# Causal attention scores without their masked columns, and gate projections placed inside an attention's loop

## The chip, the cores and the metric

The kernel runs on one core of a Trainium2 chip. Its time is device microseconds of one execution, and the time of record is the median of three. The engines are TensorE (PE, with its weight loads shown apart as PEld), VectorE (DVE), ScalarE (ACT), GpSimd (POOL) and SyncE (SP), whose queue issues nearly all DMA.

## The reference

Two blocks of two layers each work on 256 tokens of width 1024. The change is in the second block only, in its token mix, which runs once in each of the two layers: three causal attentions over one input, each with eight heads of 64, then a gated sum.

```python
def _token_mix(h, w_in, ...):
    q_a, kv_a, g_a, q_b, k_b, v_b, q_c, k_c, v_c, f_c = _split_cols(h @ w_in)
    o_a = _nsa(q_a, kv_a, g_a, ...)                 # compressed + selected + window attention
    o_b = _swa_sink(q_b, k_b, v_b, sinks, ...)      # window of 128, with a sink
    o_c = _fox(q_c, k_c, v_c, f_c, b_f)             # full causal, with a forget term
    g = jax.nn.sigmoid(h @ w_gate + b_gate).reshape(B, S, N_BRANCH, D)
    merged = g[:, :, 0] * (o_a @ w_br_a) + g[:, :, 1] * (o_b @ w_br_b) + g[:, :, 2] * (o_c @ w_br_c)
    return merged @ w_out

# in _fox, and with masks of their own in the other two:
    logits = jnp.where(s_idx[None] <= t[:, None], logits, -jnp.inf)
    p = jax.nn.softmax(logits, axis=-1)
    return jnp.einsum('bhqk,bhkd->bhqd', p, v)
```

With 256 tokens in two tiles of 128, a query of the first tile never sees a key of the second, in any of the three.

## The kernel before, in words

Every matrix product is done in three matmuls of split operands (`mm3`, L546 to L549): each float32 operand is kept as a high part and a rest, both of a rounded float32 type. A weight chunk of 128 x 1024 is loaded by SP (`advance`, L344), cast by ACT (L354) to its high part and subtracted by DVE (L356) to its rest. `Weights` holds three raw chunks and, in this part, five split ones; `make_plan` fixes the order of the chunks, and `take` and `done` hand them out and give them back. `natural` (a projection) takes four chunks at once and runs the two token tiles over them, eight `mm3` of 512 columns for each; it gives its chunks back in the second tile's pass. An activation tile in PSUM is split by `split` (ACT L536, DVE L537).

`mix` runs the token mix. Its three attentions are loops over eight units (four head pairs of two heads):

- SWA and FOX go through `simple`, and NSA through a loop of its own (L1879 to L1907).
- A unit's part `soft` computes the scores (L1685, L1686 and in FOX L1689; in NSA L1847 and L1851), the negated minimum (DVE L625), the exponentials (ACT L615, L1863) and the scaling (DVE L621, L1872).
- The loop then transposes a unit's probabilities on PE (L1710; L1883, L1884), splits them into the buffers `pts`, starts `soft` of the next unit, and multiplies the probabilities with the values by `mm3` (in NSA then L1904 for the compressed keys).

Scores and values run over all 256 keys for either query tile; the softmax reads only the valid 128 of the first tile, and the value product reads a zeroed quarter of `pts` in the place of the others.

Other work is put into these loops as filler: generators stand in a queue, and `fill(ns)` steps the first of them until its declared time is used up. In NSA the filler is the second branch (`branch_job(1)`): for each half of 512 output columns the gate projection (`natural`, evacuated by DVE L1770 and ACT L1771) and then the branch's output projection, whose result is multiplied with the gate by DVE (L1789) and added by POOL (L1790). The third branch (`branch_job(2)`) runs behind the NSA loop, with the add on DVE and, for each token tile and half, a step `last` that transposes the result on PE (L1918) and splits it for the next product (`wout`).

A scheduler then orders the instructions of each engine by priority and readiness, so that matmuls that are written later can move forward.

Of the kernel before, what the change touches and what calls it, by code (L numbers as in the profile page):

```python
# [478 lines left out]
class Kern:  # L479
# [979 lines left out]
    def mix(self, l, xh, xl, mid):  # L1459
        nc, fa, ra, d = self.nc, self.fa, self.ra, self.d  # L1460
        V, A, G, PE = nc.vector, nc.scalar, nc.gpsimd, nc.tensor
        ident = self.ident
        vec = self.load(f"vec2{l}")
# [209 lines left out]
        def simple(prep, vh, vl, paired, og, extra):  # L1673
# [5 lines left out]
            def soft(u):  # L1679
# [3 lines left out]
                for qt in range(2):  # L1683
                    qq, o = q[:, qt * P:qt * P + P], bank[:, qt * P:qt * P + S]
                    PE.matmul(o, qq, kh, start=True, stop=False)  # L1685
                    PE.matmul(o, qq, kl, start=False, stop=extra is None)  # L1686
                    if extra:
                        n = P if qt == 0 else S
                        PE.matmul(bank[:, qt * P:qt * P + n], pick[:, h:h + 1].to_broadcast([P, P]), extra[:, 0:n],  # L1689
                                  start=False, stop=True)  # L1690
                sb, ss = sr.next(), self.sm.next()
# [11 lines left out]
            for n, u in enumerate(units):  # L1703
# [7 lines left out]
                p_h, p_l = pts[n % 2]  # L1711
                self.split(bank[:, 0:384], p_h.a[:, P:], p_l.a[:, P:])
                if i == 0 and j < 3:
# [43 lines left out]

        def branch_job(b, og, last=None):
            oh = og[0].rearrange("p (k t) -> p k t", k=4)
            ol = og[1].rearrange("p (k t) -> p k t", k=4)  # L1760
            for h in range(2):
                bg = bgr.next()
                src = (1, 2, 0)[b]
                nc.sync.dma_start(bg, d[f"bgate{l}"][0:1, src * D + h * 512:src * D + h * 512 + 512]
                                  .partition_broadcast(P))
                th = {}

                def gate_evac(t, ps):
                    th[t] = thr.next()
                    V.tensor_tensor(th[t], ps, bg, ALU.add)  # L1770
                    A.activation(th[t], th[t], AF.Tanh, scale=0.5)  # L1771

                yield from self.natural(f"gate{l}", 8 * b + 4 * h, 2, xh, xl, [0, 1], gate_evac)
                cs = [self.W.take(f"br{l}", 4 * b + 2 * h + c) for c in range(2)]
                for t in range(2):
                    ps = self.pg.next()
                    tk = slice(t * P, t * P + P)
                    for k in range(4):
                        hi, lo = cs[k // 2]
                        sl = slice((k % 2) * 512, (k % 2) * 512 + 512)  # L1780
                        self.mm3(ps, oh[:, k, tk], ol[:, k, tk], hi[:, sl], lo[:, sl], k == 0, k == 3)
                        yield 640
                        if t == 1 and k % 2 == 1:
                            self.W.done()
                    ms = m[:, t, h * 512:h * 512 + 512]
                    if b == 0:
                        V.scalar_tensor_tensor(ms, th[t], 1.0, ps, ALU.add, ALU.mult)
                    else:
                        V.scalar_tensor_tensor(th[t], th[t], 1.0, ps, ALU.add, ALU.mult)  # L1789
                        (V if last else G).tensor_tensor(ms, ms, th[t], ALU.add)  # L1790
                        if last:
                            last(t, h)

# [20 lines left out]


        self.push(branch_job(1, og_c))
        W1 = 288
        slb, wib = ra.alloc(4 * W1), ra.alloc(4 * S)
# [22 lines left out]
        def soft(u):  # L1841
            j, i = u
            q, hd = heads[j][i], j + 4 * i
            bs, bw = self.ps.next(), self.ps.next()
            for qt in range(2):
                for z in range(2):
                    PE.matmul(bs[:, 160 * qt:160 * qt + W1], q[:, qt * P:qt * P + P], sl4[:, i, z],  # L1847
                              start=z == 0, stop=z == 1)
            for qt in range(2):
                for z in range(2):  # L1850
                    PE.matmul(bw[:, P * qt:P * qt + S], q[:, qt * P:qt * P + P], wi4[:, i, z],  # L1851
                              start=z == 0, stop=z == 1)
# [23 lines left out]
        for n, u in enumerate(units):  # L1876
# [3 lines left out]
            for k, (s, o, w) in enumerate(((s1, 160, 32), (s2, P, 0))):  # L1880
# [3 lines left out]
                PE.transpose(bank[0:32, 384:512], s1[:, 160 * k:160 * k + 32], ident)  # L1884
                self.split(bank[:, 0:384], pts[k][0].a[:, P:], pts[k][1].a[:, P:])
                cq, bq = slice(k * P, k * P + P), bank[0:32, 384:512]
# [5 lines left out]
            if n + 1 < 8:  # L1892
                soft(units[n + 1])
            self.fill(2500)
            if i == 0:
                self.obank = self.po.next()
            o = self.obank[:, i * S:i * S + S]
            for k in range(2):
                for kt in range(2):
                    r = slice(S - kt * S, 2 * S - kt * S)  # L1900
                    c = slice(k * P, k * P + P)
                    self.mm3(o, vsh[:, kt, c], vsl[:, kt, c], pts[k][0].a[:, r], pts[k][1].a[:, r],
                             k == 0 and kt == 0, False)
# [17 lines left out]

        self.run(branch_job(2, og_a, last))
        for b in (oga, mb, bgr, thr, vec, tiny):
            b.free()
# [38 lines left out]
```

## Time and profile before

| | us |
|---|---|
| median of three runs | 2344.83 |
| lowest, highest | 2343.74, 2349.3 |
| the profiled execution | 2346.41 |
| its span, first to last instruction | 2344.6 |

Over the span PE is busy for 96%, its weight loads for 79%, DVE for 72%, ACT for 53% and POOL for 10%. A stretch of the trace is read as busy time of each engine in it. Since the modelled end of a matmul lies behind the start of the next, the distance between starts tells more about PE's pace than the duration does. Times in the trace count from the span's start.

### The profile page before, as it was taken

What the parts mean: (1) busy time and instruction counts of PE and PEld (TensorE: products, weight loads), DVE (VectorE), ACT (ScalarE), POOL (GpSimd) and SP (SyncE); (2) the same over time, 40 slices, a digit from 0 to 9 for tenths busy, and PEclk for the clock granted to TensorE, in tenths of its full rate; (3) what the DMA queues carried; (4) which work ended last, traced back from release to release, by engine and by line L of the source; (5) the groups of instructions that cost most, each with busy time, mean ns of one, the idle gap of its engine ahead of it and who ended that gap; (6) DMA issues with size and microseconds to landing.
All of it is one profiled execution on the core that took longest, in us unless ns stands there. A gap on an engine that the chain in (4) does not pass through costs nothing.

```text
span 2344.6 us, 32027 instructions
## 1 busy us (share of the span) xinstructions
PE 2261.1 (96%) x11612; PEld 1858.8 (79%) x11612; DVE 1696.6 (72%) x3192; ACT 1249.1 (53%) x2235; POOL 244.0 (10%) x265
## 2 busy tenths in 40 slices
PE   6999899999999999999999999999999999999998
PEld 3888787787778899888877777788788877777887
DVE  6598999677689997655577897755655677897554
ACT  6385673242347864444367785444444376764452
POOL 1302200222220202200000000000000000000000
PEclk9999999999999999999999999999999999999999
DMA  8121224355443335555646435556556545445554
GB/s 321 45 82 41 75 81 135 126 165 168 134 139 110 103 132 171 179 186 180 220 137 205 138 117 173 179 188 197 189 190 219 163 153 184 144 131 179 189 190 134
DMA packets 102975, 362.98 MB, mean 155 GB/s; under 512 B 11936, under 2 KB 13088, under 8 KB 102304
## 3 DMA queue, kind: packets, MB, share of 16 engines
q1 hardware_dynamic: 102816, 360.93, 46.5%
q8 instruction: 91, 1.49, 0.3%
q14 instruction: 68, 0.56, 0.1%
HBM read 359.84 MB, written 1.05 MB: 154 GB/s over the span
## 4 chain that ended last, share of the span: by engine, by line
PE 55%; DVE 8%; ACT 4%; DMA 3%; issue 2%; POOL 1%; DVEq 0%; ACTq 0%; POOLq 0%; SPq 0%
PE bank L547 17%; PE bank L549 17%; PE bank L548 16%; DVE ra_t L356 2%; ACT ra_t L354 1%; DMA fa_t<-in_gate 1%; PE bank L1402 1%; DVE ra_t L537 1%; DVE fa_t L625 1%; DVE fa_t L1339 1%; DMA fa_t<-in_n 1%; PE bank L1265 1%; ACT ra_t L536 1%; POOL fa_t L543 0%; ACT fa_t L1863 0%
## 5 line engine op out<-in xcount | busy, mean ns | idle before, releaser
L547 PE MATMUL bank<-ra_t 128*128 128x512 f32 (+1 forms) x3216 | 1186.9, 371 | 14.3 <-DVE fa_t L786 5.0
L549 PE MATMUL bank<-ra_t 128*128 128x512 f32 (+1 forms) x3216 | 1172.8, 366 | 8.3 <-DVE ra_t L537 3.8
L548 PE MATMUL bank<-ra_t 128*128 128x512 f32 (+1 forms) x3216 | 1174.6, 367 | 3.8 <-DVE ra_t L537 1.3
L356 DVE TENSOR_TENSOR ra_t<-fa_t,ra_t 128x1024 fp32r<-128x1024 f32 x583 | 722.2, 1241 | 349.1 <-ACT ra_t L354 333.6
L354 ACT CAST ra_t<-fa_t 128x1024 fp32r<-128x1024 f32 x606 | 633.2, 1048 | 602.2 <-PE bank L549 284.5
L547 PEld LDWEIGHTS bank<-ra_t 128*128 128x128 f32 x3216 | 605.4, 189 | 129.1 <-ACT ra_t L536 15.4
L549 PEld LDWEIGHTS bank<-ra_t 128*128 128x128 f32 x3216 | 605.6, 189 | 108.7 <-DVE ra_t L537 7.3
L548 PEld LDWEIGHTS bank<-ra_t 128*128 128x128 f32 x3216 | 607.2, 189 | 103.1 <-DVE ra_t L356 5.1
L865 DVE SCALAR_TENSOR_TENSOR fa_t<-fa_t 128x512 f32<-128x512 f32 (+1 forms) x240 | 161.5, 673 | 6.0 <-ACT fa_t L863 2.8
L537 DVE TENSOR_TENSOR ra_t<-bank,ra_t 128x512 fp32r<-128x512 f32 (+5 forms) x234 | 131.2, 568 | 44.0 <-ACT ra_t L536 41.1
L536 ACT CAST ra_t<-bank 128x512 fp32r<-128x512 f32 (+5 forms) x234 | 112.8, 488 | 84.8 <-PE bank L549 33.4
L543 POOL TENSOR_TENSOR fa_t<-fa_t 128x1 f32<-128x1 f32 (+2 forms) x54 | 69.0, 1278 | 762.3 <-DVE fa_t L542 762.1
L625 DVE CUSTOM_DVE_ANT_0 fa_t<-bank,fa_t 128x256 f32<-128x256 f32 (+2 forms) x320 | 117.0, 396 | 8.7 <-PE bank L1231 1.9
L615 ACT ACTIVATE fa_t<-fa_t 128x257 f32<-128x257 f32 (+5 forms) x160 | 91.5, 574 | 21.4 <-DVE fa_t L625 20.1
L1410 ACT ACTIVATE fa_t<-bank 128x256 f32<-128x256 f32 x88 | 33.9, 385 | 112.5 <-PE bank L549 112.4
L356 POOL TENSOR_TENSOR ra_t<-fa_t,ra_t 128x1024 fp32r<-128x1024 f32 x23 | 58.0, 2520 | 276.1 <-ACT ra_t L354 273.0
L1412 DVE TENSOR_TENSOR fa_t<-fa_t,bank 128x256 f32<-128x256 f32 x88 | 36.8, 418 | 65.7 <-ACT fa_t L1410 65.5
L1184 DVE SCALAR_TENSOR_TENSOR fa_t<-fa_t 128x512 f32<-128x512 f32 x98 | 71.0, 757 | 2.3 <-DMA fa_t<-in_ada 2.0
L1053 POOL TENSOR_TENSOR fa_t<-fa_t 128x512 f32<-128x512 f32 (+1 forms) x32 | 37.3, 1172 | 154.4 <-DVE fa_t L1052 154.4
L638 DVE TENSOR_TENSOR ra_t<-bank,ra_t 64x256 fp32r<-64x256 f32 (+1 forms) x96 | 43.5, 455 | 8.3 <-ACT ra_t L637 5.3
L649 POOL CAST ra_t<-fa_t 64x256 fp32r<-64x256 f32 (+3 forms) x40 | 24.0, 606 | 241.4 <-PE bank L1597 69.9
L1863 ACT ACTIVATE fa_t<-fa_t 128x32 f32<-128x32 f32 (+2 forms) x96 | 39.0, 409 | 14.5 <-DVE fa_t L625 13.9
(218 smaller groups left out, 1701.9 us busy)
## 6 DMA issues: line engine op xcount, KB each, us to landing
fa_t<-in_f1w SPq DMA_DIRECT2D x132, 512.0 KB, 4.2
fa_t<-in_f2w SPq DMA_DIRECT2D x132, 512.0 KB, 4.3
fa_t<-in_tr SPq DMA_DIRECT2D x88, 512.0 KB, 3.5
fa_t<-in_n SPq DMA_DIRECT2D x56, 512.0 KB, 3.6
fa_t<-in_ada SPq DMA_DIRECT2D x48, 512.0 KB, 4.5
fa_t<-in_gate SPq DMA_DIRECT2D x48, 512.0 KB, 3.7
fa_t<-in_nat SPq DMA_DIRECT2D x36, 512.0 KB, 4.2
fa_t<-in_proj SPq DMA_DIRECT2D x24, 512.0 KB, 3.5
```

Source lines behind the costliest of these rows:

```text
L354: nc.scalar.copy(hi, raw)
L356: eng.tensor_tensor(lo, raw, hi.bitcast(F32), ALU.subtract)
L536: self.nc.scalar.copy(hi, src)
L537: self.nc.vector.tensor_tensor(lo, src, hi.bitcast(F32), ALU.subtract)
L543: self.nc.gpsimd.tensor_tensor(out, out, self.nhalf[:, :n], ALU.pow)
L547: mm(ps, lh, rh, start=start, stop=False)
L548: mm(ps, lh, rl, start=False, stop=False)
L549: mm(ps, ll, rh, start=False, stop=stop)
L615: nc.scalar.activation(s[:, :width or n], s[:, :width or n], AF.Exp, bias=mneg, scale=-1.0, accum_out=r)
L625: self.nc.vector.tensor_tensor_reduce(out=out, in0=a, in1=b, op0=ALU.add, op1=ALU.min, scale=-1.0, scalar=init, accum_out=acc)
L865: V.scalar_tensor_tensor(y4, src, w, y4, ALU.mult, ALU.add)
L1184: V.scalar_tensor_tensor(acc[s].a, wk, self.sc[:, kt, s:s + 1], acc[s].a, ALU.mult, ALU.add)
```

## The change

1. In all three attentions the score matmuls of the first query tile run over the 128 keys that it can see (in NSA's first product 32 compressed ones and 128), and the value product of the second key tile covers the second query tile only. `pts` shrinks to three quarters, and its zeroing goes.
2. `branch_job` is taken apart into `gate_half` and `out_half`. The two gate halves of the third branch are pushed into the queue of fillers behind the second branch, before the NSA loop, with a buffer of their own (`ga`); behind the loop only the output halves run.
3. The two `fill` calls of the NSA loop grow from 2500 and 1000 to 4500 and 2300.
4. The plan's order of weight chunks follows: the eight gate chunks of the third branch, then its four output chunks.

```diff
-        for b in range(3):
+        for b in range(2):
             ...
             for h in range(2):
                 add(f"gate{l}", 8 * b + 4 * h, 8 * b + 4 * h + 4)
                 add(f"br{l}", 4 * b + 2 * h, 4 * b + 2 * h + 2)
+        add(f"gate{l}", 16)
+        add(f"br{l}", 8)
...
-        pts = []
-        for i in range(2):
-            b = (ra.alloc(512), ra.alloc(512))
-            for z in b:
-                V.tensor_copy(z.a[:, 0:P], self.zero[:, 0:P])
-            pts.append(b)
+        pts = [(ra.alloc(3 * P), ra.alloc(3 * P)) for _ in range(2)]
...
                 for qt in range(2):
-                    qq, o = q[:, qt * P:qt * P + P], bank[:, qt * P:qt * P + S]
-                    PE.matmul(o, qq, kh, start=True, stop=False)
-                    PE.matmul(o, qq, kl, start=False, stop=extra is None)
+                    n = P if qt == 0 else S
+                    qq, o = q[:, qt * P:qt * P + P], bank[:, qt * P:qt * P + n]
+                    PE.matmul(o, qq, kh[:, :n], start=True, stop=False)
+                    PE.matmul(o, qq, kl[:, :n], start=False, stop=extra is None)
...
-                o = self.obank[:, i * S:i * S + S]
-                for kt in range(2):
-                    r = slice(S - kt * S, 2 * S - kt * S)
+                for kt, r in enumerate((slice(P, 3 * P), slice(0, P))):
+                    o = self.obank[:, i * S + kt * P:i * S + S]
                     self.mm3(o, vh[:, kt, c], vl[:, kt, c], p_h.a[:, r], p_l.a[:, r], kt == 0, kt == 1)
...
+        def gate_half(b, h, th):
+            bg = bgr.next()
+            ...
+            def evac(t, ps):
+                V.tensor_tensor(th[t], ps, bg, ALU.add)
+                A.activation(th[t], th[t], AF.Tanh, scale=0.5)
+            yield from self.natural(f"gate{l}", 8 * b + 4 * h, 2, xh, xl, [0, 1], evac)
+
+        def out_half(b, h, th, og, last=None):
+            ...                       # the rest of branch_job's loop, as it was
+
+        def branch_job(b, og):
             for h in range(2):
+                th = [thr.next(), thr.next()]
+                yield from gate_half(b, h, th)
+                yield from out_half(b, h, th, og)
...
         self.push(branch_job(1, og_c))
+        gab = fa.alloc(4 * 512)
+        ga = gab.v("p (h t c) -> p h t c", h=2, t=2)
+        for h in range(2):
+            self.push(gate_half(2, h, [ga[:, h, t] for t in range(2)]))
...
             for qt in range(2):
+                n = P if qt == 0 else S
                 for z in range(2):
-                    PE.matmul(bs[:, 160 * qt:160 * qt + W1], q[:, qt * P:qt * P + P], sl4[:, i, z],
+                    PE.matmul(bs[:, 160 * qt:160 * qt + 32 + n], q[:, qt * P:qt * P + P], sl4[:, i, z, :32 + n],
                               start=z == 0, stop=z == 1)
...
-            self.fill(2500)
+            self.fill(4500)
...
-            self.fill(1000)
+            self.fill(2300)
...
-        self.run(branch_job(2, og_a, last))
+        for h in range(2):
+            self.run(out_half(2, h, [ga[:, h, t] for t in range(2)], og_a, last))
```

What the scheduler makes of it shows at three places, all in layer 0. On PE, in the middle of the NSA loop, the transposes of a unit (from `fa_t`, into `bank_69` and `bank_68`) were followed by the next unit's scores (into `bank_66`) mixed with the unit's own values (into `bank_70`) and with filler (512 columns). Before:

```order
L547 MATMUL bank_65<-ra_t 128x512
L1883 MATMUL bank_69<-fa_t 128x128 x3
L1884 MATMUL bank_69<-fa_t 32x128
L1883 MATMUL bank_68<-fa_t 128x128 x3
L1884 MATMUL bank_68<-fa_t 32x128
L1847 MATMUL bank_66<-ra_t 128x288 x2
L547 MATMUL bank_70<-ra_t 128x256
L1847 MATMUL bank_66<-ra_t 128x288 x2
L548 MATMUL bank_65<-ra_t 128x512
```

and now:

```order
L551 MATMUL bank_65<-ra_t 128x512
L1891 MATMUL bank_69<-fa_t 128x128 x3
L1892 MATMUL bank_69<-fa_t 32x128
L1891 MATMUL bank_68<-fa_t 128x128 x3
L1892 MATMUL bank_68<-fa_t 32x128
L1854 MATMUL bank_66<-ra_t 128x160 x2
L1854 MATMUL bank_66<-ra_t 128x288 x2
L1859 MATMUL bank_67<-ra_t 128x128 x2
L1859 MATMUL bank_67<-ra_t 128x256 x2
L549 MATMUL bank_65<-ra_t 128x512
```

The values have moved away from the transposes: 24 filler matmuls now stand between the scores and them, and 12 more behind them, from the unit with index 2 on; in the first units the order is close to the old one.

On DVE, behind the NSA loop, a step of the third branch is a multiply from PSUM (L1789, now L1785), an add (L1790, now L1786) and, behind the transposes, a split (L537, now L539 of 128x4x128); L356 splits weight chunks, and L1770 is a gate's evacuation. Before:

```order
L537 TENSOR_TENSOR ra_t<-bank_70,ra_t 64x256
L1770 TENSOR_TENSOR fa_t<-bank_63,fa_t 128x512
L356 TENSOR_TENSOR ra_t<-fa_t,ra_t 128x1024
L537 TENSOR_TENSOR ra_t<-bank_70,ra_t 64x256
L1789 SCALAR_TENSOR_TENSOR fa_t<-fa_t,bank_64 128x512
L1790 TENSOR_TENSOR fa_t<-fa_t 128x512
L356 TENSOR_TENSOR ra_t<-fa_t,ra_t 128x1024
```

and now:

```order
L539 TENSOR_TENSOR ra_t<-bank_70,ra_t 64x256 x2
L1785 SCALAR_TENSOR_TENSOR fa_t<-fa_t,bank_63 128x512
L1786 TENSOR_TENSOR fa_t<-fa_t 128x512
L1785 SCALAR_TENSOR_TENSOR fa_t<-fa_t,bank_64 128x512
L356 TENSOR_TENSOR ra_t<-fa_t,ra_t 128x1024
L539 TENSOR_TENSOR ra_t<-bank_68,ra_t 128x4x128
L1786 TENSOR_TENSOR fa_t<-fa_t 128x512
L356 TENSOR_TENSOR ra_t<-fa_t,ra_t 128x1024
L1785 SCALAR_TENSOR_TENSOR fa_t<-fa_t,bank_65 128x512
```

The gate evacuations are gone from between the steps, and the steps of the four quarters follow one another directly, with 11 to 17 matmuls between their groups of transposes on PE.

On SP, the loads for the end of the NSA loop and the tail (`in_ln` is the next norm's vectors, `in_bgate` a gate's bias). Before:

```order
L344 DMA fa_t<-in_gate 128x1024 x4
L1764 DMA fa_t<-in_bgate 128x512
L344 DMA fa_t<-in_br 128x1024
L1328 DMA fa_t<-in_ln 128x1024
L344 DMA fa_t<-in_br 128x1024
```

and now:

```order
L344 DMA fa_t<-in_gate 128x1024 x4
L1758 DMA fa_t<-in_bgate 128x512
L344 DMA fa_t<-in_gate 128x1024 x4
L344 DMA fa_t<-in_br 128x1024 x2
L1330 DMA fa_t<-in_ln 128x1024
```

The second half's gate chunks have moved ahead of the first half's output chunks.

## Rows read from the trace of the kernel before

**Rows 1.** Busy by stretch: us, then PE, PEld, DVE, ACT, POOL (instructions), PEclk, DMA.
```profile
1345.00:1424.50 79.50, 76.30 (x432) 61.68 (x431) 71.85 (x243) 60.42 (x188) 6.15 (x4) 1.00 0.39 127
1424.50:1455.00 30.50, 30.18 (x141) 24.40 (x141) 23.40 (x29) 15.96 (x20) 0.00 (x0) 1.00 0.58 196
2020.00:2099.00 79.00, 75.77 (x427) 61.24 (x426) 71.31 (x243) 59.98 (x188) 6.16 (x4) 1.00 0.39 126
2099.00:2125.00 26.00, 25.87 (x119) 20.69 (x120) 19.58 (x24) 13.54 (x17) 0.00 (x0) 1.00 0.60 190
```
**Rows 2.** PE in order of time, a dense stretch: start us, duration us, instruction.
```profile
1338.06 0.39 PE L547 MATMUL bank<-ra_t 128*128 128x512 f32 x1
...
1339.88 0.39 PE L549 MATMUL bank<-ra_t 128*128 128x512 f32 x1
```
**Rows 3.** PE in order of time, scores of one FOX unit in layer 0.
```profile
1301.28 0.28 PE L1686 MATMUL bank<-ra_t 128*128 128x256 f32 x1
1301.40 0.22 PE L1689 MATMUL bank<-ra_t 128*128 128x128 f32 x1
1301.46 0.33 PE L1685 MATMUL bank<-ra_t 128*128 128x256 f32 x1
1301.63 0.28 PE L1686 MATMUL bank<-ra_t 128*128 128x256 f32 x1
1301.75 0.28 PE L1689 MATMUL bank<-ra_t 128*128 128x256 f32 x1
```
**Rows 4.** PE's weight loads in order of time, the same scores, first and last.
```profile
1301.16 0.19 PEld L1686 LDWEIGHTS bank<-ra_t 128*128 128x128 f32 x1
...
1301.75 0.19 PEld L548 LDWEIGHTS bank<-ra_t 128*128 128x128 f32 x1
```
**Rows 5.** PE groups by shape, 1345 to 1424.5 us: count, busy, mean ns, idle before.
```profile
L547 PE MATMUL bank<-ra_t 128*128 128x512 f32 x63 | 25.3, 401 | 0.0
L549 PE MATMUL bank<-ra_t 128*128 128x512 f32 x63 | 24.9, 396 | 0.0
L548 PE MATMUL bank<-ra_t 128*128 128x512 f32 x62 | 24.4, 393 | 0.0
L547 PE MATMUL bank<-ra_t 128*128 128x256 f32 x32 | 9.8, 307 | 0.3 <-DVE ra_t L537 0.2
...
L1883 PE MATMUL bank<-fa_t 128*128 128x128 f32 x48 | 7.7, 277 | 2.2 <-DVE fa_t L1872 2.2
L1847 PE MATMUL bank<-ra_t 128*128 128x288 f32 x32 | 6.3, 304 | 0.0
L1851 PE MATMUL bank<-ra_t 128*128 128x256 f32 x32 | 5.4, 282 | 0.0
L1884 PE MATMUL bank<-fa_t 128*32 128x128 f32 x16 | 4.4, 273 | 0.0
L1904 PE MATMUL bank<-ra_t 128*128 128x256 f32 x8 | 2.9, 360 | 0.2
L1659 PE MATMUL bank<-fa_t 128*128 128x128 f32 x12 | 2.2, 282 | 0.5 <-ACT ra_t L665 0.4
```
**Rows 6.** PE's waits in the same stretch: us, times, longest.
```profile
PE bank L1883 <- DVE fa_t L1872: 2.2, 3, 0.9
```
**Rows 7.** PE in order of time, a wait in the SWA stage of layer 0.
```profile
1246.93 0.35 PE L1685 MATMUL bank<-ra_t 128*128 128x256 f32 x1 [1.04 <-DVE fa_t L625]
```
**Rows 8.** DVE groups by shape in the tail, 1424.5 to 1455 us.
```profile
L356 DVE TENSOR_TENSOR ra_t<-fa_t,ra_t 128x1024 fp32r<-128x1024 f32 x12 | 14.7, 1222 | 5.2 <-ACT ra_t L354 4.8
...
L1790 DVE TENSOR_TENSOR fa_t<-fa_t 128x512 f32<-128x512 f32 x4 | 2.8, 688 | 0.1
L1789 DVE SCALAR_TENSOR_TENSOR fa_t<-fa_t,bank 128x512 f32<-128x512 f32 x4 | 2.7, 681 | 0.8 <-PE bank L549 0.8
```

More of the change, by code (lines that the diff above doesn't have):

```diff
@@ L1683, in soft @@
                 for qt in range(2):
-                    qq, o = q[:, qt * P:qt * P + P], bank[:, qt * P:qt * P + S]
-                    PE.matmul(o, qq, kh, start=True, stop=False)
-                    PE.matmul(o, qq, kl, start=False, stop=extra is None)
+                    n = P if qt == 0 else S
+                    qq, o = q[:, qt * P:qt * P + P], bank[:, qt * P:qt * P + n]
+                    PE.matmul(o, qq, kh[:, :n], start=True, stop=False)
+                    PE.matmul(o, qq, kl[:, :n], start=False, stop=extra is None)
                     if extra:
-                        n = P if qt == 0 else S
-                        PE.matmul(bank[:, qt * P:qt * P + n], pick[:, h:h + 1].to_broadcast([P, P]), extra[:, 0:n],
-                                  start=False, stop=True)
+                        PE.matmul(o, pick[:, h:h + 1].to_broadcast([P, P]), extra[:, 0:n], start=False, stop=True)
                 sb, ss = sr.next(), self.sm.next()
@@ L1711, in simple @@
                 p_h, p_l = pts[n % 2]
-                self.split(bank[:, 0:384], p_h.a[:, P:], p_l.a[:, P:])
+                self.split(bank[:, 0:384], p_h.a, p_l.a)
                 if i == 0 and j < 3:
@@ L1756, in mix @@
         thr = Ring(fa, 512, 2)
-        def branch_job(b, og, last=None):
+        def gate_half(b, h, th):
+            bg = bgr.next()
+            src = (1, 2, 0)[b]
+            nc.sync.dma_start(bg, d[f"bgate{l}"][0:1, src * D + h * 512:src * D + h * 512 + 512]
+                              .partition_broadcast(P))
+            def evac(t, ps):
+                V.tensor_tensor(th[t], ps, bg, ALU.add)
+                A.activation(th[t], th[t], AF.Tanh, scale=0.5)
+            yield from self.natural(f"gate{l}", 8 * b + 4 * h, 2, xh, xl, [0, 1], evac)
@@ L1759, in branch_job @@
+        def out_half(b, h, th, og, last=None):
             oh = og[0].rearrange("p (k t) -> p k t", k=4)
             ol = og[1].rearrange("p (k t) -> p k t", k=4)
-            for h in range(2):
[L1762 to L1792, printed above, removed]
@@ new lines, in out_half @@
+            cs = [self.W.take(f"br{l}", 4 * b + 2 * h + c) for c in range(2)]
+            for t in range(2):
+                ps = self.pg.next()
+                tk = slice(t * P, t * P + P)
+                for k in range(4):
+                    hi, lo = cs[k // 2]
+                    sl = slice((k % 2) * 512, (k % 2) * 512 + 512)
+                    self.mm3(ps, oh[:, k, tk], ol[:, k, tk], hi[:, sl], lo[:, sl], k == 0, k == 3)
+                    yield 640
+                    if t == 1 and k % 2 == 1:
+                        self.W.done()
+                ms = m[:, t, h * 512:h * 512 + 512]
+                if b == 0:
+                    V.scalar_tensor_tensor(ms, th[t], 1.0, ps, ALU.add, ALU.mult)
+                else:
+                    V.scalar_tensor_tensor(th[t], th[t], 1.0, ps, ALU.add, ALU.mult)
+                    (V if last else G).tensor_tensor(ms, ms, th[t], ALU.add)
+                    if last:
+                        last(t, h)
@@ L1845, in soft @@
             for qt in range(2):
+                n = P if qt == 0 else S
                 for z in range(2):
-                    PE.matmul(bs[:, 160 * qt:160 * qt + W1], q[:, qt * P:qt * P + P], sl4[:, i, z],
+                    PE.matmul(bs[:, 160 * qt:160 * qt + 32 + n], q[:, qt * P:qt * P + P], sl4[:, i, z, :32 + n],
                               start=z == 0, stop=z == 1)
             for qt in range(2):
+                n = P if qt == 0 else S
                 for z in range(2):
-                    PE.matmul(bw[:, P * qt:P * qt + S], q[:, qt * P:qt * P + P], wi4[:, i, z],
+                    PE.matmul(bw[:, P * qt:P * qt + n], q[:, qt * P:qt * P + P], wi4[:, i, z, :n],
                               start=z == 0, stop=z == 1)
@@ L1884, in mix @@
                 PE.transpose(bank[0:32, 384:512], s1[:, 160 * k:160 * k + 32], ident)
-                self.split(bank[:, 0:384], pts[k][0].a[:, P:], pts[k][1].a[:, P:])
+                self.split(bank[:, 0:384], pts[k][0].a, pts[k][1].a)
                 cq, bq = slice(k * P, k * P + P), bank[0:32, 384:512]
@@ L1898, in mix @@
             for k in range(2):
-                for kt in range(2):
-                    r = slice(S - kt * S, 2 * S - kt * S)
+                for kt, r in enumerate((slice(P, 3 * P), slice(0, P))):
                     c = slice(k * P, k * P + P)
-                    self.mm3(o, vsh[:, kt, c], vsl[:, kt, c], pts[k][0].a[:, r], pts[k][1].a[:, r],
+                    self.mm3(o[:, kt * P:], vsh[:, kt, c], vsl[:, kt, c], pts[k][0].a[:, r], pts[k][1].a[:, r],
                              k == 0 and kt == 0, False)
@@ L1920, in last @@
             self.split(bank.rearrange("p (k t) -> p k t", k=4), m4[:, 0][c], m4[:, 1][c])
-        self.run(branch_job(2, og_a, last))
-        for b in (oga, mb, bgr, thr, vec, tiny):
+        for h in range(2):
+            self.run(out_half(2, h, [ga[:, h, t] for t in range(2)], og_a, last))
+        for b in (oga, gab, mb, bgr, thr, vec, tiny):
             b.free()
```

## The prediction

> **What bounds the kernel now.** I read the busy shares by stretch first. The last attention of a layer's second block (the loop over eight units that ends at L1907, here called the NSA stage) takes 79.5 us in layer 0 and 79.0 in layer 1; the third branch behind it (the tail) takes 30.5 and 26 up to the cuts chosen [rows 1]. In the NSA stage PE is busy for 76.3 of 79.5 us, but DVE for 71.85, which is 90%; in the tail PE is busy for 30.2 of 30.5 and DVE for 23.4, 77%. So the stage has the two engines side by side near their limits, and the tail is PE's alone.
>
> Matmul ends are modelled, so busy PE says little about how much of it is a stream. I therefore count. A 512-column matmul starts every 0.2275 us when nothing stands in the way (eight steps in 1.82 us) [rows 2]. Those of 256 columns start every 0.12, and the weight loads in front of them every 0.118 (five steps in 0.59) [rows 3, 4]. With 0.2275 for the 512-column ones, 0.118 for all of 256 columns and fewer and 0.135 for 288 (0.12 and 32 columns at the slope below), the matmuls of the NSA stage of layer 0 [rows 5] come to 188 x 0.2275 + 212 x 0.118 + 32 x 0.135 = 42.8 + 25.0 + 4.3 = 72.1 us. **The stage holds 7.4 us in which PE doesn't stream.** Layer 1 has five instructions fewer and is 0.5 us shorter, so about the same; 15 us in both. Part of it has a name: the transposes of a unit (L1883) wait for the scaled probabilities (DVE, L1872), 2.2 us in three waits, the longest 0.9 us [rows 6]; the rest are restarts behind the splits, which the modelled durations cover up.
>
> The Trainium skill ("Trainium Kernel Development and Optimization", section Performance Expectations) says to judge PE by the busy share of weight loads and not of matmuls. By that the stage would have 79.5 - 61.7 = 17.8 us of room [rows 1], and both stages 35; the trace doesn't bear that out, since a load also sits idle under a 512-column stream that is itself the limit.
>
> **The narrower matmuls.** Per unit, the SWA and FOX attentions narrow two score and three value matmuls from 256 to 128 columns: 5 x 8 units x 2 attentions x 2 layers = 160. NSA narrows two scores from 288 to 160, two from 256 to 128 and six value matmuls: 10 x 8 x 2 = 160. By columns each would save 128 x (0.2275 - 0.12)/256 = 0.054 us, 17 us in all. But FOX already has a 128-column matmul in a row of 256-column ones (L1689, sixteen of them): it starts 0.06 us before its successor, and the successor then takes 0.17 instead of 0.12 [rows 3]. The four matmuls of that row take 0.47 us, where four at 0.12 would take 0.48. What sets the pace is the weight load, one per matmul, at 0.118 whatever the columns. So 288 of them save 0.005 to 0.01 us, and the 32 from 288 columns 0.017: 1.9 to 3.4 us. I take **2.5 us**, of which 0.8 in each NSA stage, with 0 as the far end. They can't cost anything themselves: the loads are the same and the streams shorter. On DVE eight clearing copies disappear from stretches where PE leads; nothing.
>
> The narrowing also lets the scheduler put the SWA stage in another order, with the same instructions. One wait there, of a score matmul for a softmax's first pass (L625), is 1.04 us long [rows 7]; such a wait may go or double. I take 0, and 1 us either way for each layer.
>
> **The moved gates.** Two halves of four gate chunks, 96 matmuls of 512 columns per layer, now stand in the filler, and the filler calls grow from 3.5 to 6.8 us per unit. This is less of a move than it reads: of the 144 matmuls of the second branch and the 96 gates, 240 in all, 188 already ran inside the NSA stage [rows 5], because the scheduler pulled gates of the third branch forward. So 52 more enter: 52 x 0.2275 = 11.8 us of PE work, which the tail loses. Time is won only where the work goes into the 7.4 us without a stream.
>
> With no wait left, the stage would take 72.1 + 11.8 - 0.8 = 83.1 us where stage and moved work take 79.5 + 11.8 = 91.3 now. But DVE comes along: 52/12 = 4.3 more chunks to split at 1.22 us (L356) and three more gate evacuations at 0.68 (like L1789, the same size) [rows 8] make 71.85 + 5.3 + 2.0 = 79.2 us, 95% of 83.1. If PE can only go so fast that DVE stays at today's 90.4%, the stage takes 79.2/0.904 = 87.6, and the waits that go are 91.3 - 87.6 - 0.8 = 2.9 us. So between 2.9 and 7.4 us of waits go per layer. The new order says where: from the third unit on, the transposes of a unit are followed at once by the next scores, then by 24 filler matmuls, then by the values, then by 12 more, where they used to be followed by values that wait for the split. Such a unit takes PE 36 x 0.2275 + 29 x 0.118, some 11.6 us, against 79.2/8 = 9.9 on DVE, so it should not wait. In units 0 to 2 the order is still nearly the old one, transposes soon after scores, and there the waits on L1872 stay. I leave 3.5 us of waits per layer, so **3.9 us go, twice: 7.8 us**. This is nearer to the end by DVE's share, which is the row for the same engine in the same stage.
>
> SP's queue carries the same loads; the last four br chunks now come behind eight gate chunks in a row. Each is held back by a split that frees its buffer, and there are five split chunks ahead of PE; I cost it at nothing, since 2.7 us of matmuls (12 x 0.2275) stand on each chunk. The cover is gone where DVE falls behind with the splits, and then it is the 95% above that speaks.
>
> **The tail.** What is left is four steps of 12 matmuls and four transposes, 12 x 0.2275 + 4 x 0.118 = 3.2 us each. Each step's chain is DVE's: multiply 0.68, add 0.69, then transposes, then a split of the same size, 0.69, and in the new order about one chunk split, 1.22, between them [rows 8]: 3.28 us. Before, gates stood between the halves and hid this. Now DVE is late by some 0.1 us per step, and the first step also waits for the last unit's output to be split: **0.5 us per layer, 1 us lost**. The bounds: nothing lost; or a second chunk split in every step, 4 x 1.22 x 2 = 9.8.
>
> **Sum.** -2.5 - 7.8 + 1.0 = -9.3 us. The profiled execution took 2346.4 us with a span of 2344.6 and the runs have a median of 2344.8; I take the same off each: 2335.5.
>
> **Rivals.**
> (a) Narrow matmuls pay by columns: -17 for them instead of -2.5, in all 2344.8 - 17 - 6.8 = 2321. For it speaks that 320 of them stand next to one another in pairs, which L1689 never did; against it that the loads of [rows 4] keep 0.118 straight through the narrow one. It decides if two narrow ones in a row start less than 0.1 us apart. The Trainium skill ("TensorE: Matmul & The Clock Gate", section on the back-to-back issue gap) gives about 81 ns for a pair of load and 128-column matmul; by it 320 x 0.039 = 12.5 us would be saved instead of 2.5. The row says 0.118, and the same sentence's 131 ns for 512 columns is not seen here either (0.2275).
> (b) DVE takes the gain back: the chunk splits in the NSA stage come late, and gate matmuls wait for L356 where transposes waited for L1872. Then only the narrowing and 1 to 2 us of waits are left: 2344.8 - 3.5 = 2341. For it: 95%.
> (c) The tail loses its cover outright: transposes directly behind their chain, so that PE waits for multiply, add and a chunk split, 0.68 + 0.69 + 1.22 = 2.6 us, in each of eight steps, 21 us, less 10.3 gained: 2355, slower than before. It decides when DVE needs more than 3.2 + 1.3 us a step, that is with two or three chunk splits in it. Against it: the new order has one in most steps and 11 to 17 matmuls between the groups of transposes.
> (d) The waits all go: 14.8 instead of 7.8, 2344.8 - 16.3 = 2328.5.
>
> **How the numbers follow.** A measurement can tell 0.3%, 7 us, from no change: faster means below 2337.8. My forecast (2331 to 2340) has 0.58, (a) 0.06, (b) 0.20, (c) 0.06, (d) 0.10. Of the forecast about three quarters lie below 2337.8; with (a) and (d) that makes 0.6 faster. The rest of the forecast and (b) make 0.35 within 0.3%, and (c) 0.05 slower. The range leaves out (a), (c) and the edges: 2328 to 2343.
>
> **What would show it.** Right: in the NSA stage nearly all L1883 waits beyond unit 2 gone, about 240 matmuls of 512 columns inside it and the stage about 87 us long; the score and value matmuls of 128 columns starting every 0.11 to 0.12 us; the tail about 14 us. Wrong: pairs of narrow matmuls at 0.06 us (then a); PE waiting for L356 in the NSA stage with DVE above 95% (b); L1918 waiting more than 1 us each time (c).

## The result, and the profile after

The changed kernel is slower: 2367.4 us (median; 2365.4 to 2375.25) beside 2345.32 for the kernel before, a ratio of 1.0098, 95% interval 1.0072 to 1.0124. The profiled execution took 2366.89 us with a span of 2365.1, 20.5 us more than before's. I had forecast 2335.5 and a range up to 2343.

Line numbers have moved by a few: `mm3` is L549 to L551, `split` L538 and L539, scores L1684 to L1687 (NSA L1854, L1859), transposes of SWA and FOX L1707, of NSA L1891 and L1892, the pair transposes of `q_pair` L1657 (L1659 before), copies to `pc` L1895 to L1897, scaling L623 and L1880, and the compressed values L1911.

First the stretches, as busy time of the engines: us, then PE, PEld, DVE, ACT, POOL (instructions), PEclk, DMA. SWA (from 10 us ahead of its first score) and FOX (up to the first NSA score) of layer 0, first before, then after:

```profile
1211.70:1291.50 79.80, 75.78 (x420) 59.27 (x418) 62.36 (x145) 61.07 (x137) 5.90 (x17) 1.00 0.57 185
1291.50:1350.80 59.30, 57.80 (x309) 45.82 (x308) 48.09 (x128) 42.03 (x97) 1.86 (x5) 1.00 0.43 142
...
1208.60:1291.10 82.50, 75.88 (x416) 57.92 (x414) 62.37 (x143) 60.24 (x135) 5.73 (x17) 1.00 0.55 184
1291.10:1354.40 63.30, 59.34 (x313) 47.03 (x312) 49.85 (x129) 43.20 (x99) 1.88 (x5) 1.00 0.38 127
```

And of after the NSA stage and the tail of layer 0, cut as in [rows 1] (from 5.8 us ahead of the first NSA score):

```profile
1348.60:1447.60 99.00, 89.25 (x494) 74.24 (x493) 79.95 (x252) 68.25 (x196) 5.11 (x4) 0.98 0.42 138
1447.60:1464.00 16.40, 16.40 (x80) 13.13 (x79) 13.87 (x19) 8.23 (x11) 0.00 (x0) 1.00 0.46 153
```

SWA and FOX, which I had costed at nothing, are 2.7 and 4.0 us longer, and NSA with its tail 99.0 + 16.4 = 115.4 where [rows 1] have 79.5 + 30.5 = 110.0: 5.4 us longer. That is 12.1 in layer 0; layer 1 repeats it within 0.5 us. Twice 12 are 24, and 3 of them don't show in the span, because the untouched work ahead of SWA was 3.1 us quicker in this execution (SWA begins at 1208.6 instead of 1211.7): the kernel before had two stretches at a lower clock there (granted 0.56 from 464.5 to 468.0 us, 0.55 from 587.4 to 590.8) that this execution lacks.

Where PE waited shows in its waits (us, times, longest). FOX of layer 0, before:

```profile
PE bank L1710 <- DVE fa_t L621: 0.8, 2, 0.6
```

FOX after, and behind the cut NSA after, both in layer 0:

```profile
PE bank L1707 <- DVE fa_t L623: 1.8, 2, 1.4
PE bank L1657 <- ACT ra_t L667: 0.7, 2, 0.4
PE bank L1684 <- ACT ra_t L667: 0.7, 2, 0.4
...
PE bank L1657 <- ACT ra_t L1897: 4.6, 3, 2.3
PE bank L1891 <- DVE fa_t L1880: 2.1, 3, 0.9
PE bank L549 <- ACT ra_t L538: 1.0, 1, 1.0
```

All of PE's waits in FOX add up to 3.8 us now and to 1.4 before, and five matmuls of 512 columns (1.1 us) moved from SWA into FOX; together that is most of its 4.0 us.

The waits of NSA's transposes for the scaling, whose end was the point of the move, are as long as before (2.1 us, [rows 6] have 2.2). New is a wait of the pair transposes for the copies to `pc`, 4.6 us. The longest of them in order of time (start, duration, instruction), on PE, ACT and DVE:

```profile
1406.30 0.39 PE L550 MATMUL bank<-ra_t 128*128 128x512 f32 x1
1409.02 0.44 PE L1657 MATMUL bank<-fa_t 128*128 128x128 f32 x2 [2.34 <-ACT ra_t L1897]
...
1404.41 2.00 ACT L354 CAST ra_t<-fa_t 128x1024 fp32r<-128x1024 f32 x2
1406.43 0.86 ACT L538 CAST ra_t<-bank 128x384 fp32r<-128x384 f32 x2
1408.72 0.25 ACT L1897 CAST ra_t<-bank 32x128 fp32r<-32x128 f32 x1
...
1405.49 1.22 DVE L356 TENSOR_TENSOR ra_t<-fa_t,ra_t 128x1024 fp32r<-128x1024 f32 x1 [0.65 <-ACT ra_t L354]
1406.75 0.69 DVE L1785 SCALAR_TENSOR_TENSOR fa_t<-fa_t,bank 128x512 f32<-128x512 f32 x1
1407.36 1.02 DVE L539 TENSOR_TENSOR ra_t<-bank,ra_t 128x384 fp32r<-128x384 f32 x2
```

The unit's transposes (from 1403.56) fill both PSUM banks of the ring `pt`, and the pair transposes, written right behind them, need the first of the two again. Its readers are a split and the three copies to `pc`, and these stand on ACT behind two weight casts and on DVE behind a weight split and a gate's multiply. In the new order only the scores and five filler matmuls lie between. The wait costs more than its length; PE's clock behind it (the same columns as the stretches):

```profile
1409.00:1411.00 2.00, 1.98 (x7) 1.65 (x8) 1.94 (x12) 1.95 (x10) 0.00 (x0) 0.64 0.20 72
1411.00:1413.00 2.00, 2.00 (x6) 1.52 (x6) 1.87 (x5) 1.62 (x7) 0.00 (x0) 0.51 0.00 0
1413.00:1416.00 3.00, 3.00 (x18) 2.57 (x17) 2.17 (x9) 0.00 (x0) 0.00 (x0) 1.00 0.53 175
```

Behind this wait the granted clock is at its lower level, 1.2 GHz, for some 3.4 us; nine matmuls of 512 columns take 3.6 us there, where [rows 2] give 9 x 0.2275 = 2.05, so 1.6 us more. (The last section has waits as long as this one that no lower clock followed.)

### The profile page after: what moved, and what is told of

The parts are those of the page before. It is cut to its first block, busy times and chain, and to the rows that moved or that the text cites. A ratio compares the mean times of both kernels' runs of the same rounds, so it can differ in the third digit from the quotient of the medians.

```text
span 2365.1 us, 32045 instructions
## 1 busy us (share of the span) xinstructions
PE 2258.1 (95%) x11612; PEld 1857.9 (79%) x11612; DVE 1697.5 (72%) x3184; ACT 1248.1 (53%) x2235; POOL 243.7 (10%) x265
## 4 chain that ended last, share of the span: by engine, by line
PE 51%; DVE 11%; ACT 5%; DMA 3%; issue 3%; POOL 1%; DVEq 0%; ACTq 0%; POOLq 0%; SPq 0%
PE bank L551 16%; PE bank L549 16%; PE bank L550 16%; DVE ra_t L356 3%; ACT ra_t L354 2%; DVE ra_t L539 1%; DVE fa_t L627 1%; PE bank L1404 1%; DVE fa_t L867 1%; DVE ra_t L640 1%; DMA fa_t<-in_br 1%; DVE fa_t L623 1%; ACT fa_t L1871 1%; DVE fa_t L1341 1%; DMA fa_t<-in_n 1%
## 5 line engine op out<-in xcount | busy, mean ns | idle before, releaser
L549 PE MATMUL bank<-ra_t 128*128 128x512 f32 (+1 forms) x3216 | 1184.0, 370 | 18.7 <-DVE fa_t L788 5.0
L551 PE MATMUL bank<-ra_t 128*128 128x512 f32 (+1 forms) x3216 | 1174.0, 366 | 9.1 <-DVE ra_t L539 3.8
L356 DVE TENSOR_TENSOR ra_t<-fa_t,ra_t 128x1024 fp32r<-128x1024 f32 x583 | 720.3, 1238 | 368.9 <-ACT ra_t L354 353.5
L549 PEld LDWEIGHTS bank<-ra_t 128*128 128x128 f32 x3216 | 605.7, 189 | 129.6 <-ACT ra_t L538 16.3
L551 PEld LDWEIGHTS bank<-ra_t 128*128 128x128 f32 x3216 | 606.6, 189 | 110.6 <-DVE ra_t L539 7.3
L539 DVE TENSOR_TENSOR ra_t<-bank,ra_t 128x512 fp32r<-128x512 f32 (+5 forms) x234 | 130.3, 566 | 43.9 <-ACT ra_t L538 42.4
L538 ACT CAST ra_t<-bank 128x512 fp32r<-128x512 f32 (+5 forms) x234 | 112.2, 487 | 81.9 <-PE bank L551 27.4
L627 DVE CUSTOM_DVE_ANT_0 fa_t<-bank,fa_t 128x256 f32<-128x256 f32 (+2 forms) x320 | 115.4, 395 | 7.2 <-PE bank L1233 1.9
L356 POOL TENSOR_TENSOR ra_t<-fa_t,ra_t 128x1024 fp32r<-128x1024 f32 x23 | 57.4, 2494 | 276.6 <-ACT ra_t L354 273.5
L639 ACT CAST ra_t<-bank 64x256 fp32r<-64x256 f32 (+1 forms) x96 | 37.4, 392 | 13.3 <-DVE ra_t L640 4.0
```

What stands on the lines that cost most here:

```text
L356: eng.tensor_tensor(lo, raw, hi.bitcast(F32), ALU.subtract)
L538: self.nc.scalar.copy(hi, src)
L539: self.nc.vector.tensor_tensor(lo, src, hi.bitcast(F32), ALU.subtract)
L549: mm(ps, lh, rh, start=start, stop=False)
L551: mm(ps, ll, rh, start=False, stop=stop)
L627: self.nc.vector.tensor_tensor_reduce(out=out, in0=a, in1=b, op0=ALU.add, op1=ALU.min, scale=-1.0, scalar=init, accum_out=acc)
```

## The experiments

**Which part costs what.** Four kernels take the change apart. Theory A: the narrow matmuls cost the time through the order that the scheduler makes of them. B: the move of the gates does. C: the narrow matmuls are slow in themselves. For NSA, A1 names the wait of the pair transposes, A2 the narrow matmuls.

`narrow_simple` is the kernel before with, in `simple` alone:

```diff
-                    PE.matmul(o, qq, kh, start=True, stop=False)
+                    PE.matmul(o, qq, kh[:, :n], start=True, stop=False)
...
-                    r = slice(S - kt * S, 2 * S - kt * S)
+                for kt, r in enumerate((slice(2 * P, 4 * P), slice(P, 2 * P))):
+                    o = self.obank[:, i * S + kt * P:i * S + S]
```

> The kernel before, with the narrow score and value matmuls in SWA and FOX alone; NSA and the gates as they were. Theory A (the narrow matmuls bring another order on PE, in which the units of SWA and FOX stand closer together, with less filler between a softmax and its transposes): the whole loss of these two stages is here. In the traces of before and after the way from 10 us ahead of the first SWA score to the first NSA score is 139.0 and 145.8 us in layer 0, 138.7 and 145.5 in layer 1, so this kernel takes 2345 + 13.6 = 2359 us, with waits of the transposes for the scaling of 1.4 to 1.8 us per stage. Theory B (the gates' move costs it all: chunks come in another order, and the loads and splits are late): the same as before or 1 to 3 us less, 2342 to 2345. Theory C (narrow matmuls are slow in themselves): their starts lie more than 0.12 us apart.

`after_wide_simple` is the changed kernel with this hunk turned round.

> The changed kernel with SWA and FOX set back to wide matmuls; NSA is narrow, and the gates stand in the filler. Theory A: the two stages take 139 us again, and the loss of NSA and tail is left. From the first NSA score to 12 us behind the last transposes it was 114.6 us before and 119.9 after in layer 0, so this kernel takes 2345 + 2 x 5.3 = 2355 to 2356 us, with three waits per layer of L1657's transposes (the next pair of queries) for the copies to pc, 4.6 us. Theory B (the gates' move costs it all): 2366 to 2368, as the changed kernel.

`gates` is the kernel before with parts 2 to 4 of the change and none of part 1.

> The kernel before with the gates moved and the larger fills, all matmuls wide as before. In its order the pair transposes of the queries stand 11 filler matmuls behind a unit's transposes once and 7 filler matmuls behind the scores once, where the changed kernel has 4 and 5. Theory A1 (in NSA the loss is the wait of these transposes for a PSUM bank that the copies to pc release last): the waits are shorter, one to 1.3 us per layer less each, and the loss is about half, 2345 + 5 = 2350. Theory A2 (the loss of NSA comes with its narrow matmuls, as in SWA and FOX): 2345 or less, down to my first forecast for the moved gates, 2338. Theory B (the move costs it all): 2366.

`after_q_late` is the changed kernel with

```diff
-            if i == 0 and j < 3:
-                heads[j + 1] = q_pair(qa, j + 1)
             if n + 1 < 8:
                 soft(units[n + 1])
             self.fill(4500)
+            if i == 0 and j < 3:
+                heads[j + 1] = q_pair(qa, j + 1)
```

> The changed kernel, with the call of q_pair (the two transposes L1657 and their split for the next pair of queries) written behind the fill of 4500 and not ahead of the next scores; the same instructions. Theory A1: the three waits of L1657 per layer (4.6 us) go, and with them the 3.4 us at a granted clock of about 0.5 behind the longest of them in layer 0 (1.7 us lost there): 2 x 6.3 = 12.6 us less than the changed kernel, 2355. Rival (ACT and DVE are behind with the splits in any case): the same time is waited at the values for their split, 2366 to 2368.

Measured, as ratios to the kernel before: `narrow_simple` 1.0058 (1.0043 to 1.0073), `after_wide_simple` 1.0033 (1.0022 to 1.0043), `gates` 0.9984 (0.9974 to 0.9994), `after_q_late` 1.0057 (1.0042 to 1.0072). So 14 of the 22 us come with the narrow matmuls of SWA and FOX, and 8 with NSA and the gates together. The move by itself is a gain, so B falls, and the 8 must come with NSA's narrow matmuls, which speaks for A2. A1 is right as well, but for part of it. The NSA loop of layer 0 in the changed kernel, then with `q_pair` behind the fill:

```profile
1354.40:1447.30 92.90, 83.55 (x467) 69.90 (x466) 75.69 (x245) 63.70 (x185) 5.11 (x4) 0.98 0.40 130
...
1358.70:1446.30 87.60, 83.33 (x467) 70.04 (x466) 75.22 (x245) 63.31 (x185) 5.16 (x4) 0.98 0.44 138
```

That is 5.3 us (in layer 1 it is 4.1), where I had expected 6.3. Some of it is waited at the values for their split instead, as the rival had it: 1.7 us in one wait of layer 0, 1.0 in the changed kernel.

The narrow matmuls alone in NSA, without the gates:

> The kernel before with narrow matmuls in NSA alone. In its order 78 filler matmuls stand between the last NSA product and the third branch's first transposes where 30 stood before, so 48 fewer lie inside the loop. Theory A (the narrow matmuls make the scheduler pack a loop too closely, here too): slower, by waits of the values for their split and of the transposes for the scaling, some 3 to 6 us per layer: 2352 to 2358. Rival (in NSA the narrow matmuls cost something only together with the moved gates): 2343 to 2346.

1.0058 (1.0036 to 1.0081), 14 us and above my range; the rival falls. That is more than the 8 us of NSA and the gates together, so next to narrow matmuls too the moved gates seem to take time off and not to add any (from the first NSA score to the last transposes of layer 0: 109.7 us here, 106.5 in `after_wide_simple`; the intervals of the two ratios overlap). The parts alone, 14 and 14 us lost and 4 gained, add up to 24; the whole change loses 22. Its waits in the NSA loop of layer 0:

```profile
PE bank L1885 <- DVE fa_t L1874: 6.2, 6, 2.6
```

Here the transposes wait 6.2 us for the scaling where [rows 6] have 2.2; in this order 78 filler matmuls, not 30, are left behind the loop.

**Order or width.** The scheduler was then held to an order of my choice, by edges between successive instructions of a queue:

```diff
+def issue_order(tc):
+    by = {i.name: i for i in tc.nc.cur_bb.bb.instructions}
+    info = mybir.DependencyInfo(mybir.DependencyClass.NoSync, mybir.DependencyReason.DATA)
+    ...                # for each pair a, b of neighbours in a table of instruction numbers:
+            tc.add_manual_dep(by[f"I-{b}"], f"I-{a}", info, reason="issue order")
...
     Kern(ctx, tc, d, out).emit()
+    issue_order(tc)
```

The matmuls of `narrow_simple` in the old order, and the wide ones in the order of `narrow_simple`:

> The kernel with narrow matmuls in SWA and FOX alone (2361 us), but with the scheduler held to the order of the kernel before, on PE, DVE and ACT, by edges of issue order. Theory A (the order alone costs the time): SWA and FOX take 139 us again, and the time is that of the kernel before or 1 to 3 us less, 2344 to 2347. Theory C (the narrow matmuls cost it, through their own pace or through what a shorter score leaves uncovered): 2357 to 2361.

> The other corner: the kernel before, all matmuls wide, held to the order that the scheduler makes of the kernel with narrow matmuls in SWA and FOX. Theory A: as slow as that kernel or 1 to 3 us slower, 2360 to 2364. Theory C: 2346.

Wide matmuls in the new order cost 1.0056 (1.0036 to 1.0076), as much as the narrow ones. The narrow ones in the old order took 1.0032 (1.0023 to 1.0042), halfway, which fits neither theory. One cause showed in its trace. SP (start, duration, load) and an ACT cast of it, then the same in the kernel before:

```profile
1250.51 0.42 SPq L1749 DMA_DIRECT2D fa_t<-in_t  x1
1252.60 8.53 SPq L344 DMA_DIRECT2D fa_t<-in_n  x4
1258.47 1.04 ACT L354 CAST ra_t<-fa_t 128x1024 fp32r<-128x1024 f32 x1 [3.13 <-DMA fa_t<-in_n]
...
1254.44 0.33 SPq L344 DMA_DIRECT2D fa_t<-in_n  x1
1255.19 0.70 SPq L1751 DMA_DIRECT2D fa_t<-in_t  x1
1258.73 1.05 ACT L354 CAST ra_t<-fa_t 128x1024 fp32r<-128x1024 f32 x1 [1.56 <-DMA fa_t<-in_n]
```

SP had been left free, and the 1 MB of `in_t` went ahead of a weight chunk instead of behind it. So SP was held as well, and the reverse was tried on the kernel before:

> Narrow matmuls in SWA and FOX, with PE, DVE, ACT and now SP's queue too held to the order of the kernel before. In the run before this one SP was free, and put the load of t5 (128 x 2048, 1 MB) ahead of one chunk of in_n instead of behind it; there ACT waited 3.1 us for that chunk (1.6 us in the kernel before), and the split that PE's values wait for stood behind it. Theory A (order alone, SP's included): SWA and FOX take 139 us, the whole 2343 to 2347. Theory C (the narrow matmuls cost something themselves): 2353 as in the run before.

> The kernel before, wide, PE, DVE and ACT held to their own order, and SP's queue alone in the order of the run with narrow matmuls in the old order: t5 ahead of one in_n chunk, and a gate's bias ahead of one in_cw chunk, once per layer. Theory A: the 7 us that were left there are these two places, so 2350 to 2354. Theory C: 2346.

1.0009 (0.9999 to 1.0018) and 1.0025 (1.0014 to 1.0035): the place of that load (with that of one gate's bias, which moved with it) is worth some 6 us by itself. FOX still took 61.1 us. There the softmax's first pass on DVE (L625), which the tables had missed, stood behind two splits. With it in the table:

> Narrow matmuls in SWA and FOX; every queue held to the order of the kernel before, now with the softmax's first pass (DVE L625) too, which the two runs before left free: there FOX still took 61.1 us instead of 59.2, and in its middle the first pass of the next scores stood behind two splits instead of ahead of them. Theory A: SWA and FOX take 139 us, ratio 0.998 to 1.000. Theory C (narrow matmuls cost something themselves): FOX stays at 61, ratio 1.001 or more.

1.0001 (0.9992 to 1.0011), and FOX, wide in the new order, then narrow in the old:

```profile
1296.20:1359.90 63.70, 59.68 (x314) 47.38 (x313) 50.03 (x130) 43.29 (x99) 1.87 (x5) 1.00 0.37 125
...
1294.50:1353.70 59.20, 57.42 (x308) 45.42 (x307) 48.06 (x128) 41.92 (x96) 1.85 (x5) 1.00 0.44 143
```

59.2 us is the kernel before to a tenth. The order makes the difference, and the width none that these runs can tell (0.1% either way). C falls, and so does any gain. What the edges themselves cost was not measured apart: no run holds the kernel before to its own order on every queue. (SWA varies between executions of one kernel, 79.6 and 81.4 us in the two profiles of the wide kernel below; the second has a granted clock of 0.58 from 1284.5 to 1288.5 us, the first 1.00 throughout. So SWA is judged by the ratios, FOX and NSA by their stretches too.)

**The same for NSA.** All matmuls wide, in the order that came with the narrow ones:

> All matmuls wide, gates moved, but the order of every queue held to the one that the scheduler makes with narrow matmuls in NSA (that kernel took 2355.0; with its own order the wide one takes 2343.0). Theory A for NSA (the narrow matmuls cost time there by the order alone): 2355 to 2358, with three waits of the pair transposes per layer, 4 to 5 us. Rival (the narrow matmuls uncover DVE's chain, whatever the order): 2343 to 2346.

1.0045 (1.0029 to 1.0062), where the same instructions in their own order took 0.9984. The NSA loop of layer 0 in their own order, then in this one, with its longest entry among the waits:

```profile
1350.00:1437.00 87.00, 84.01 (x472) 70.43 (x471) 77.43 (x245) 63.12 (x185) 5.14 (x4) 1.00 0.44 139
...
1352.20:1446.30 94.10, 84.98 (x467) 70.77 (x466) 75.79 (x245) 63.90 (x185) 5.11 (x4) 0.98 0.41 129
...
PE bank L1661 <- ACT ra_t L1901: 4.9, 2, 3.4
```

PE's order is that of `after_wide_simple` to the instruction, but the first pass on DVE was not in this table either and stands elsewhere in places. The longest wait of the pair transposes is 3.4 us here and 2.3 there, so the loss is brought back by the order, not matched wait by wait.

**A better kernel.** With the gates moved and `q_pair` behind the fill, wide and narrow:

> All matmuls wide, gates moved, larger fills (2343.0 us), and q_pair written behind the fill of 4500. The two waits of L1661 (the pair transposes) for the copies to pc were 1.8 us in layer 0. Theory A1: they go, in both layers, 3 us less, 2340. Rival (DVE at 89% of the stage takes it back): 2343.

> Everything that the change does (all narrow matmuls, gates moved, larger fills), with q_pair behind the fill and the order of every queue held to that of the wide kernel of the same text (2340.2). Theory A: the narrow matmuls now bring what their work is worth, 0 to 3.5 us (320 of them at 0.11 instead of 0.12 us), so 2337 to 2340, faster than both kernels by over 0.2%. Rival (stages that are bound by DVE's chain take nothing from shorter matmuls, or lose): 2340 to 2350.

> The wide kernel with the gates moved and q_pair behind the fill, again, so that it stands beside the narrow one on one chip: 0.9978 as before.

> All that the change does, with q_pair behind the fill and every queue, the first pass included, held to the order of the wide kernel of the same text. Theory A: the narrow matmuls are worth 0 to 3.5 us against the wide kernel of this call, ratio to before 0.9965 to 0.998, and no stage is longer than in the wide one. Theory C: 0.998 to 1.000, slower than the wide one.

The wide kernel took 0.9978 (0.9968 to 0.9987), and measured again 0.9964 (0.9952 to 0.9977), 2338.0 us beside 2347.05. The narrow one took 0.999 (0.998 to 0.9999) with the first pass left free, and 0.9967 (0.9954 to 0.9979) with the whole order held, level with the wide one. So the wide kernel beats both kernels of this case, and needs no table. Its NSA stretch, its tail, and its only waits of note in the stretch:

```profile
1349.70:1435.00 85.30, 83.31 (x473) 70.34 (x472) 77.47 (x245) 62.62 (x185) 6.10 (x4) 1.00 0.43 142
1435.00:1448.80 13.80, 13.80 (x67) 11.12 (x68) 11.75 (x17) 7.58 (x10) 0.00 (x0) 1.00 0.41 138
...
PE bank L549 <- ACT ra_t L538: 1.1, 1, 1.1
PE bank L1895 <- DVE fa_t L1884: 0.8, 1, 0.8
```

**Spacing.** Last, narrow matmuls in SWA and FOX with `fill(1300)` and `fill(700)` of `simple` raised to 1900 and 1300, and no order held:

> Narrow matmuls in SWA and FOX, no order held, but the fills of these two loops raised from 1300 and 700 to 1900 and 1300, so that more filler is written between a unit's scores and the next transposes; 57 filler matmuls are then left behind the FOX loop, as in the kernel before, where the narrow one leaves 78. Theory A with spacing as the mechanism: a good part of the 14 us comes back, 2347 to 2354. If only the exact order of the queues helps: 2358 to 2362.

1.0025 (1.0015 to 1.0034), 2352.9 us: some 8 of the 14 us are back. In layer 0 the way from the first SWA score to the first NSA score takes 132.4 us, in `narrow_simple` 138.3, in the kernel before 129.1. So a good part of the loss goes when more filler stands between a softmax and its transposes. But most of this is in SWA, where part of it is the clock (`narrow_simple` has a granted clock of 0.50 from 1285.8 to 1292.6 us in its profile, this run 1.00 throughout). FOX takes 61.9 us, where `narrow_simple` has 62.7 and the kernel before 59.3, though as many matmuls stand behind it as before. What holds the rest of FOX's loss, beyond the order as a whole, is not shown.

## Why the prediction was wrong, point by point

- **The failed step is the scheduler's new order**: "I take 0, and 1 us either way for each layer", for SWA. By the stretches it is 2.7 us in SWA and 4.0 in FOX, and by the ratio of `narrow_simple` 14 us in all. I priced it from one wait of SWA [rows 7] and didn't follow the new order through FOX at all. There 57 filler matmuls stood behind the loop before and 78 now, so 21 were gone from inside it, and with them a lead of PE over the softmax; that this lead is the cause is argued, and the run with larger fills bears it out for FOX only in part. That the order as a whole is the cause is shown: 1.0056 for wide matmuls in it, 1.0001 for narrow ones in the old.
- **The same step failed in NSA.** I gave its narrow matmuls 0.8 us of gain per layer and no new order; alone they cost 14 us in both layers (`narrow_nsa`).
- **Another failed step is in the moved gates**: from "transposes of a unit are followed at once by the next scores, then by 24 filler matmuls, then by the values" I concluded that such a unit should not wait. The pair transposes stood among these 24 in two such units of a layer, and in an earlier one, and need a PSUM bank that the unit itself has just filled. The bank has its row only in the code: a ring of two. Writing them behind the fill took 5.3 and 4.1 us off the two layers' loops.
- **The gates' worth was sized too high for the change as it stands.** I had put 7.8 us for the waits less 1.0 for the tail, 6.8. Without the narrow order the move brings 0.16%, 4 us (1 to 6 by the interval); what the forecast left out is the wait of the pair transposes, which stays 1.8 us in layer 0 there. With these out of the way it brings 0.22 and 0.36%, 5 and 8 us, about what I had forecast. The end by DVE's share is borne out there: cut as in [rows 1], DVE is busy for 81.68 of 91.10 us, 89.7%, where I had taken 90.4%. The 52 matmuls that were to enter were too few, though: the loop holds 166 of 512 columns before, 228 in the changed kernel and 234 in `gates`, 62 and 68 more.
- **The tail was right**: 15 us from the last compressed values to the last transposes, forecast 14, and PE is busy for all of it. Rival (c), the only one on the slow side, has its place there and did not happen.
- **The narrow matmuls were right in their price and too high in their sum.** As far as starts show, the weight load sets the pace. Values of one FOX unit, narrow (start, duration), which answer [rows 3]:

```profile
1298.49 0.28 PE L551 MATMUL bank<-ra_t 128*128 128x256 f32 x1
1298.61 0.22 PE L549 MATMUL bank<-ra_t 128*128 128x128 f32 x1
1298.67 0.27 PE L550 MATMUL bank<-ra_t 128*128 128x128 f32 x1
1298.78 0.27 PE L551 MATMUL bank<-ra_t 128*128 128x128 f32 x1
1298.89 0.45 PE L549 MATMUL bank<-ra_t 128*128 128x512 f32 x1
```

Behind the step of 0.06, which goes with a wide one ahead, narrow ones start every 0.11 us. Rival (a) is out. The Trainium skill's 81 ns for such a pair ("TensorE: Matmul & The Clock Gate", section on the back-to-back issue gap) is not seen here either. Of the 2.5 us nothing can be told from zero: 1.0001 in SWA and FOX, 0.9967 beside 0.9964 in all.
- **Rival (b)** had the right place, NSA, and the wrong cause: DVE's share of the loop fell, from 67.33 of 73.40 us to 75.69 of 92.90, because PE waited for a bank; what came late was the split of one unit, behind casts and a gate's multiply, not the chunk splits as a whole.
- Open stays by what rule the scheduler packs the loops closer when matmuls get narrower; the runs show that it does and what it costs, in three loops.

## What to carry to other kernels

Where a scheduler orders the queues, an edit that changes an instruction's size is an edit of the order, and its price is read from the new order of every stage that holds it, not from the instruction. Before filler is moved, follow each small step between two pieces of it to the buffer that it reuses, and ask who reads that last. If a change has a part that shortens work on an engine whose pace is set elsewhere, time it apart from the part that moves work: here the first gave nothing and took the second with it.

## What the runs showed of the hardware that I had not expected

- Whether PE's clock fell behind a wait did not go by the length of the wait alone. In the changed kernel one of 2.34 us was followed by about 3.4 us at the lower clock (0.64 and 0.51 granted on average in the rows above), which cost 1.6 us more than the wait, and one of 1.79 us earlier in the same stage was not (1.00 behind it). But in `after_wide_simple` the same wait, as long, was not either, nor one of 2.64 us in `narrow_nsa`; and in `after_q_late` a shorter one was. First `after_wide_simple`, the wait and the clock behind it, then `after_q_late`:

```profile
1404.33 0.44 PE L1661 MATMUL bank<-fa_t 128*128 128x128 f32 x2 [2.33 <-ACT ra_t L1903]
1404.40:1407.00 2.60, 2.60 (x13) 2.18 (x14) 2.51 (x13) 2.52 (x13) 0.00 (x0) 1.00 0.23 87
...
1441.22 0.47 PE L549 MATMUL bank<-ra_t 128*128 128x256 f32 x1 [1.70 <-ACT ra_t L538]
1441.20:1445.00 3.80, 3.78 (x15) 3.01 (x15) 2.93 (x5) 1.71 (x4) 0.00 (x0) 0.55 0.83 271
```

- One load of 1 MB a single place earlier in SP's queue, ahead of a weight chunk of 0.5 MB, cost the program 0.25%, some 3 us each time (one gate's bias moved with it). In that run, `before_t5_early`, a value matmul waits 2.94 us for its split, which stands behind the late cast on ACT; in the kernel before PE's waits of this kind in SWA are 0.4 us. The granted clock behind the wait is 0.57 for 4 us, so part of the 3 us is the clock.
